# Right operands of a Strassen product summed in PSUM by identity passes, in a macaron block

## The chip, the cores and the metric

One core of one Trainium2 chip runs the kernel. The metric is the device time of one execution in microseconds (us); the time of a kernel is the median of its runs. A profile is one more execution, recorded by the hardware profiler; its span is the time from the first to the last recorded work.

## The reference

One layer on x of 1024 frames x 1024 channels, float32. Each feed-forward has 2816 inner channels.

```python
x = x + 0.5 * swiglu(rmsnorm(x, ff1_norm), ff1_w_gate, ff1_w_up, ff1_w_down)
h = rmsnorm(x, mix_norm)
...                      # gMLP and stick-breaking attention on h, merged, projected
x = x + m @ w_out
x = x + 0.5 * swiglu(rmsnorm(x, ff2_norm), ff2_w_gate, ff2_w_up, ff2_w_down)
return rmsnorm(x, final_norm)
```

`swiglu` is `(silu(x @ w_gate) * (x @ w_up)) @ w_down`, `rmsnorm` divides each row by its root mean square and multiplies by a gain.

## The kernel before

Every float32 product is made of three passes over operands split into a high and a low part (fp32r): high x high, high x low, low x high. A form is such a pair of parts; `form` (L152 to 157) makes one with a cast on ScalarE (L155) and a subtraction (L156), `put` (L186 to 191) makes one inside a larger tile, with the cast at L190 and the subtraction at L191.

The feed-forward (`ffn`) computes x @ w by a Strassen-Winograd scheme with seven products over 2 x 2 blocks. The right operand is the normed, transposed x: block B11 and B21 for rows 0 to 511 (the first and the second half of the channels), B12 and B22 for rows 512 to 1023, and four sums, T1 = B12 - B11, T2 = B22 - T1, T3 = B22 - B12, T4 = T2 - B21. Eight row tiles t of 128 rows are normed (`normed`, `rstd`), transposed on TensorE (`transposed`, L182) into two PSUM banks and written as forms: tiles 0 to 3 by `lo_forms` into B11 and B21, tiles 4 to 7 by `hi_forms` into T1 to T4 and B22. In the second feed-forward tiles 0 to 3 are formed by the mixer before it, at its end.

`hi_forms` first adds the high and the low part of B11 and B21 back together on GpSimd (two tiles "keep", L206), and then makes the four sums on VectorE, the first two out of PSUM (L209, L210), the others from SBUF (L213, L216). Of the five puts GpSimd does the subtraction of three (T1, T3, T4), VectorE of two (T2, B22).

A head is the part of an inner block f that needs B11 and B21 alone: two products of 12 passes each, into the banks b (from B11) and a (from B21); `head_end` adds them (L282, L283) and leaves b, into which the tail goes on accumulating. Four heads are computed between the tiles. Then come the tails, five products each, over T2, T1, T3, T4 and B22, for 22 inner blocks. Their left sums s1 to s4 (`sums`, from L163 on) are made by VectorE from the weights.

The down part multiplies by w_down with a second scheme; sums go through DRAM. Its last loop (`last`) runs products j = 0 to 10 into four banks A, one per tile t, of which the last five (j = 6 to 10) are done tile by tile; after each tile comes a sum (L490) and `after`, which norms a finished row tile. In the first feed-forward `after` also returns the transposing step `finish` (run as f() later, out of the list `lo`), in the second it stores the result.

In the stretches with the tiles 0 to 7 the order of TensorE and of the DMA queue (SyncE) is the order of the code (`manual_schedule`), in the last down loop that of TensorE; everything else is ordered by a planner that simulates the engines. All PSUM banks of a feed-forward come from one pool of 8. The parameter `offload` of `normed` says how many of a norm's two halves are multiplied by the gain on GpSimd (L116) and scaled on ScalarE (L120), the others being done on VectorE in one go (L122). With offload 2 the squares (L104) are written to a PSUM bank, otherwise to the norm's own first tile. The inverse root is a power on GpSimd (L108).

Of the kernel before, what the change touches and what calls it, by code (L numbers as in the profile page):

```python
# [7 lines left out]
F32 = mybir.dt.float32  # L8
# [5 lines left out]
P = 128  # L14
# [18 lines left out]
class Kernel:  # L33
# [77 lines left out]
    def normed(self, x, gain, tiles, offload):  # L111

        nc = self.nc
        far = [i for i in range(2) if i >= 2 - offload]
        for i in far:
            nc.gpsimd.tensor_tensor(tiles[i], x[i], gain[i], op=ALU.mult)  # L116
        r = self.rstd(x, self.psum("p3", "sq") if offload == 2 else tiles[0])
        for i in range(2):
            if i in far:
                nc.scalar.activation(tiles[i], tiles[i], AF.Copy, scale=r)  # L120
            else:
                nc.vector.scalar_tensor_tensor(tiles[i], x[i], r, gain[i], op0=ALU.mult, op1=ALU.mult)  # L122
# [10 lines left out]
    def norm_t(self, x, t, gain, h, offload=1):  # L133
# [3 lines left out]
        self.normed(x, gain, xns, offload)  # L137
# [39 lines left out]
    def transposed(self, xn):  # L177
        ps = []
        for i in range(2):
            p = self.psum("p2", "nt")  # L180
            for k in range(4):
                self.nc.tensor.transpose(p[:, k * P:(k + 1) * P], xn[i][:, k * P:(k + 1) * P], self.ident)  # L182
            ps.append(p)
# [15 lines left out]

    def hi_forms(self, t, xn, T, tmp):  # L200
        tt, pt = self.nc.vector.tensor_tensor, self.nc.gpsimd.tensor_tensor
        c, keep = (t % 4) * P, []
        for name in ("B11", "B21"):
            keep.append(tmp("keep", 2))
            hi, lo = (T[name][:, :, part, c:c + P].bitcast(F32) for part in range(2))
            pt(keep[-1].rearrange("p (k c) -> p k c", k=4), hi, lo, op=ALU.add)  # L206
        n = self.transposed(xn)
        t1, t2, t3, t4 = (tmp("t", 4) for _ in range(4))
        tt(t1, n[0], keep[0], op=ALU.subtract)  # L209
        tt(t2, n[1], t1, op=ALU.subtract)  # L210
        self.put(T["T2"], t, t2, tt)
        self.put(T["T1"], t, t1, pt)
        tt(t3, t2, keep[0], op=ALU.subtract)  # L213
        self.put(T["T3"], t, t3, pt)
        self.put(T["B22"], t, n[1], tt)
        tt(t4, t2, keep[1], op=ALU.subtract)  # L216
        self.put(T["T4"], t, t4, pt)

    def ffn(self, xsrc, gain_src, wg, wu, wd, before, after, T=None):
# [13 lines left out]
        with ExitStack() as outer:  # L233
# [16 lines left out]
            with tc.tile_pool(name="tp", bufs=3, reuse_waits="tile") as tp, tc.tile_pool(name="pg", bufs=1, reuse_waits="tile") as pg:  # L250
# [18 lines left out]
                def head(f, sub=None):  # L269
                    gate = weights(wg, f)  # L270
                    return [gate, [wform(g, sub) for g in gate], self.psum("ps", "pb"), None]

                def head_part(h, cs=slice(0, HALF)):
                    first = cs.start == 0
                    h[3] = h[3] or self.psum("ps", "pa")
                    passes(h[2], h[1][0], "B11", first, True, cs)
                    passes(h[3], h[1][1], "B21", first, True, cs)
# [8 lines left out]
                with tc.tile_pool(name="pre", bufs=1, reuse_waits="tile") as pre, tc.manual_schedule(engines={mybir.EngineType.PE, mybir.EngineType.SP}):  # L286
# [9 lines left out]
                    def norm(t):  # L296
                        xn = [tmp("xn", 4) for _ in range(2)]
                        self.normed(cut(x[t]), cut(gain), xn, 1)
# [5 lines left out]
                    if ready:  # L304
                        heads[0], heads[1] = head(0), head(1)
# [4 lines left out]
                    else:  # L310
# [102 lines left out]
            with tc.tile_pool(name="pb", bufs=1, reuse_waits="tile") as pb:  # L413
# [61 lines left out]
                with tc.manual_schedule(engines={mybir.EngineType.PE}):  # L475
                    lo = []
                    last(range(3), range(4))
# [3 lines left out]
                    for t in (0, 1):  # L481
                        lo.append(after(t, cut(x[t]), cut(gain), 2))
                    last(range(3, 5), range(4))
                    for f in lo:
                        f and f()
                    lo = [after(t, cut(x[t]), cut(gain), 2) for t in (2, 3)]
                    last(range(5, 6), range(4))
                    for t in range(4):
                        last(range(6, nj), [t], t == 0)
                        tt(xh(t + 4, 0), xh(t + 4, 0), A[t], op=ALU.subtract)  # L490
                        lo.append(after(t + 4, cut(x[t + 4]), cut(gain), 1))
                        f = lo.pop(0)
                        f and f()
# [213 lines left out]
    def run(self):  # L707
        nc, tc, a, ctx = self.nc, self.tc, self.a, self.ctx
        self.ident = self.const.tile([P, P], F32, name="ident")
        make_identity(nc, self.ident)  # L710
        self.neghalf = self.const.tile([P, 1], F32, name="neghalf")
# [11 lines left out]
        def after(t, x, gain, offload):  # L723
            for i in range(2):
                nc.sync.dma_start(out=xmid[t * P:(t + 1) * P, i * HALF:(i + 1) * HALF], in_=x[i])
            return self.norm_t(x, t, gain, hm, offload)
# [12 lines left out]
        def after3(t, x, gain, offload):  # L739
            xo = [self.np_.tile([P, HALF], F32, tag="xn", bufs=XNF, name="xo") for _ in range(2)]  # L740
            self.normed(x, gain, xo, offload)
# [5 lines left out]
    def mixer(self, xmid, xres, ydram, bgate):  # L747
# [7 lines left out]
        with tc.tile_pool(name="u2", bufs=42, reuse_waits="tile") as self.up, tc.tile_pool(name="np2", bufs=3, reuse_waits="tile") as self.np_:  # L755
# [56 lines left out]
            def after2(t):  # L812
                for i in range(2):
                    nc.sync.dma_start(out=xres[t * P:(t + 1) * P, i * HALF:(i + 1) * HALF], in_=x[t][i])
                if t < 4:
                    xn[t] = [self.utile("xn") for _ in range(2)]
                    self.normed(x[t], gain, xn[t], 1)
# [46 lines left out]
```

## Time and profile before

| | us |
|---|---|
| median of 3 runs (2554.43 to 2556.69) | 2554.93 |
| profiled execution | 2552.09 |
| span of its profile | 2550.3 |
| TensorE busy | 2429.8 |
| VectorE busy | 1716.0 |
| ScalarE busy | 1054.4 |
| GpSimd busy | 391.5 |

Matmuls are pipelined, and their ends are modelled: a pass of 512 columns is listed with 0.39 us, and the next one starts 0.23 us after it. The first feed-forward lies from 0 to about 720 us, with its tiles 0 to 7 up to about 76 us and its down part from about 420 us; the mixer follows to about 1868 us; the second feed-forward has its tiles 4 to 7 from there to about 1921 us. In the views PE is TensorE (PEld its weight loads), DVE is VectorE, ACT ScalarE, POOL GpSimd, SP SyncE; L171 to L173 are the three passes of a feed-forward product. In brackets behind a row of a timeline stands how long the engine was idle before it and what ended that.

### The profile page before, as it was taken

What the parts mean: (1) busy time and instruction counts of PE and PEld (TensorE: products, weight loads), DVE (VectorE), ACT (ScalarE), POOL (GpSimd) and SP (SyncE); (2) the same over time, 40 slices, a digit from 0 to 9 for tenths busy, and PEclk for the clock granted to TensorE, in tenths of its full rate; (3) what the DMA queues carried; (4) which work ended last, traced back from release to release, by engine and by line L of the source; (5) the groups of instructions that cost most, each with busy time, mean ns of one, the idle gap of its engine ahead of it and who ended that gap; (6) DMA issues with size and microseconds to landing.
All of it is one profiled execution on the core that took longest, in us unless ns stands there. A gap on an engine that the chain in (4) does not pass through costs nothing.

```text
span 2550.3 us, 33259 instructions
## 1 busy us (share of the span) xinstructions
PE 2429.8 (95%) x12188; PEld 2060.4 (81%) x12188; DVE 1716.0 (67%) x2605; ACT 1054.4 (41%) x2004; POOL 391.5 (15%) x538
## 2 busy tenths in 40 slices
PE   5899999999899999999999999999978999999998
PEld 4688888778798888888888988888857888887886
DVE  6877776565648888887666555135778777775655
ACT  5433333343546666665522222222343333333534
POOL 6100000000214444443300000000150000000003
PEclk9899999999999999999999999999999999999999
DMA  4454544775421212122111111123345535537653
GB/s 141 138 175 158 173 148 153 265 262 191 153 60 42 59 42 59 42 59 51 34 57 49 55 62 59 50 79 128 120 140 159 183 132 175 168 130 292 236 182 132
DMA packets 252771, 318.33 MB, mean 125 GB/s; under 512 B 14912, under 2 KB 172096, under 8 KB 252608
## 3 DMA queue, kind: packets, MB, share of 16 engines
q1 hardware_dynamic: 252608, 316.21, 38.3%
q8 instruction: 96, 1.57, 0.3%
q14 instruction: 67, 0.55, 0.1%
HBM read 227.55 MB, written 80.22 MB: 121 GB/s over the span
## 4 chain that ended last, share of the span: by engine, by line
PE 85%; DVE 5%; DMA 4%; issue 1%; ACT 1%; SPq 0%; POOL 0%; POOLq 0%; DVEq 0%; ACTq 0%
PE pj L67 7%; PE pj L68 7%; PE pj L69 7%; PE pd L171 7%; PE pd L172 7%; PE pd L173 7%; PE pb L171 4%; PE pb L172 4%; PE pb L173 4%; PE av L598 3%; PE tr L591 2%; PE pv L67 2%; PE pv L69 2%; PE pv L68 2%; PE pe L171 2%; PE pe L172 2%
## 5 line engine op out<-in xcount | busy, mean ns | idle before, releaser
L156 DVE TENSOR_TENSOR wf<-raw,wf 128x512 fp32r<-128x512 f32 x276 | 192.0, 717 | 121.3 <-ACT wf L155 121.2
L155 ACT CAST wf<-raw 128x512 fp32r<-128x512 f32 x280 | 166.2, 620 | 259.7 <-PE pd L173 128.4
L67 PE MATMUL pj<-h,wf 128*128 128x512 f32 x640 | 253.7, 396 | 5.3 <-DVE q L74 5.3
L68 PE MATMUL pj<-h,wf 128*128 128x512 f32 x640 | 252.9, 395 | 0.0
L69 PE MATMUL pj<-h,wf 128*128 128x512 f32 x640 | 252.2, 395 | 0.0
L574 DVE TENSOR_TENSOR_SCAN kp<-kp 128x128 f32<-128x128 f32 (+7 forms) x128 | 181.1, 1421 | 39.9 <-POOL kp L572 38.5
L57 DVE TENSOR_TENSOR wf<-raw,wf 128x1024 fp32r<-128x1024 f32 x88 | 108.3, 1231 | 143.8 <-ACT wf L56 143.3
L155 ACT CAST wf<-ws 128x512 fp32r<-128x512 f32 x176 | 106.6, 621 | 201.4 <-DVE ws L164 97.9
L56 ACT CAST wf<-raw 128x1024 fp32r<-128x1024 f32 x88 | 92.8, 1055 | 219.0 <-PE pj L68 116.7
L171 PE MATMUL pb<-T,wf 128*128 128x512 f32 x352 | 137.6, 391 | 34.2 <-ACT wf L155 34.2
L116 POOL TENSOR_TENSOR xn<-x,gain 128x512 f32<-128x512 f32 x16 | 23.0, 1463 | 883.4 <-DVE x L450 469.3
L578 POOL TENSOR_TENSOR bt<-bt,kp 128x512 f32<-128x512 f32 (+4 forms) x128 | 131.4, 1027 | 141.0 <-DVE kp L574 109.3
L67 PE MATMUL pv<-wf,h 128*128 128x256 f32 x512 | 145.2, 286 | 2.1 <-ACT vg L641 2.1
L67 PEld LDWEIGHTS pj<-h,wf 128*128 128x128 f32 x640 | 121.9, 190 | 30.0 <-DVE q L74 6.0
L69 PE MATMUL pv<-wf,h 128*128 128x256 f32 x512 | 145.3, 284 | 0.0
L68 PE MATMUL pv<-wf,h 128*128 128x256 f32 x512 | 145.1, 284 | 0.0
L69 PEld LDWEIGHTS pj<-h,wf 128*128 128x128 f32 x640 | 121.6, 190 | 25.1 <-DVE wf L57 0.2
L68 PEld LDWEIGHTS pj<-h,wf 128*128 128x128 f32 x640 | 121.7, 190 | 24.1
L172 PE MATMUL pb<-T,wf 128*128 128x512 f32 x352 | 137.5, 391 | 0.0
L173 PE MATMUL pb<-T,wf 128*128 128x512 f32 x352 | 136.8, 389 | 0.0
L172 PE MATMUL pd<-wf 128*128 128x512 f32 x344 | 134.6, 391 | 1.8 <-DVE wf L156 1.8
L171 PE MATMUL pd<-wf 128*128 128x512 f32 x344 | 132.8, 393 | 3.5 <-ACT wf L155 2.1
(215 smaller groups left out, 6600.2 us busy)
## 6 DMA issues: line engine op xcount, KB each, us to landing
raw<-in_ff_w_down_dram SPq DMA_DIRECT2D x66, 512.0 KB, 6.3
raw<-in_w_in_dram SPq DMA_DIRECT2D x56, 512.0 KB, 3.9
raw<-in_ff_w_gate_dram SPq DMA_DIRECT2D x52, 512.0 KB, 4.7
raw<-in_ff_w_up_dram SPq DMA_DIRECT2D x44, 512.0 KB, 6.2
f_t2t<-as SPq DMA_DIRECT2D x22, 512.0 KB, 3.2
f_a11a<-act SPq DMA_DIRECT2D x44, 256.0 KB, 4.4
f_s2s<-as SPq DMA_DIRECT2D x22, 512.0 KB, 2.7
f_s3s<-as SPq DMA_DIRECT2D x22, 512.0 KB, 5.7
```

Of the source, the lines that this page charges most:

```text
L56: nc.scalar.copy(hi, raw)
L57: (nc.gpsimd if early else nc.vector).tensor_tensor(lo, raw, hi.bitcast(F32), op=ALU.subtract)
L67: mm(ps, lhsT=lh, rhs=rh, start=first, stop=False)
L68: mm(ps, lhsT=lh, rhs=rl, start=False, stop=False)
L69: mm(ps, lhsT=ll, rhs=rh, start=False, stop=last)
L155: self.nc.scalar.copy(f[:, 0, :], src)
L156: (sub or self.nc.vector.tensor_tensor)(f[:, 1, :], src, f[:, 0, :].bitcast(F32), op=ALU.subtract)
L171: mm(ps, lhsT=lh, rhs=rh, start=first, stop=False, skip_group_check=True)
L172: mm(ps, lhsT=lh, rhs=rl, start=False, stop=False, skip_group_check=True)
L173: mm(ps, lhsT=ll, rhs=rh, start=False, stop=last, skip_group_check=True)
L574: nc.vector.tensor_tensor_scan(rev, rev, rev, 1.0, op0=ALU.mult, op1=ALU.bypass)
L578: eng.tensor_tensor(bt[:, :n], bt[:, :n], kp[:, i * HALF + 1:i * HALF + 1 + n], op=ALU.mult)
```

## The change

`hi_forms` no longer sums on VectorE. GpSimd makes one difference, diff = xn[1] - xn[0] (B22 - B12 before the transposes), TensorE transposes it into a third bank d (T3), and the other sums are made inside the banks by passes with a plus or minus identity over the forms of B11 and B21 (`plus`, two passes of 512 columns each): the bank of B12 minus B11 is T1, d plus B11 is T2, and after T2 has been put, d minus B21 is T4. All five puts read PSUM and have their subtraction on VectorE. `second` and `third` are these later steps; the heads are cut into their two products and placed between them, two of them moved by one tile in the first feed-forward. The subtractions of the head weights' forms go to GpSimd. Norms lose `offload`: always one half on GpSimd and ScalarE, the other on VectorE. In the last down loop norms 0 and 1 stand ahead of the eight adds (L479, L480), norm 2 ahead of j = 5, norm 3 ahead of j = 6, and the transposes follow one at a time.

```diff
+    def plus(self, ps, sign, form, t):
+        c = (t % 4) * P
+        for part in range(2):
+            self.nc.tensor.matmul(ps, lhsT=self.unit[sign], rhs=form[:, :, part, c:c + P], start=False, stop=True, skip_group_check=True)
     def hi_forms(self, t, xn, T, tmp):
-        tt, pt = self.nc.vector.tensor_tensor, self.nc.gpsimd.tensor_tensor
-        c, keep = (t % 4) * P, []
-        for name in ("B11", "B21"):
-            keep.append(tmp("keep", 2))
-            hi, lo = (T[name][:, :, part, c:c + P].bitcast(F32) for part in range(2))
-            pt(keep[-1].rearrange("p (k c) -> p k c", k=4), hi, lo, op=ALU.add)
-        n = self.transposed(xn)
-        t1, t2, t3, t4 = (tmp("t", 4) for _ in range(4))
-        tt(t1, n[0], keep[0], op=ALU.subtract)
-        tt(t2, n[1], t1, op=ALU.subtract)
-        self.put(T["T2"], t, t2, tt)
-        self.put(T["T1"], t, t1, pt)
-        tt(t3, t2, keep[0], op=ALU.subtract)
-        self.put(T["T3"], t, t3, pt)
-        self.put(T["B22"], t, n[1], tt)
-        tt(t4, t2, keep[1], op=ALU.subtract)
-        self.put(T["T4"], t, t4, pt)
+        tt = self.nc.vector.tensor_tensor
+        diff = tmp("diff", 2)
+        self.nc.gpsimd.tensor_tensor(diff, xn[1], xn[0], op=ALU.subtract)
+        b12, b22 = self.transposed(xn)
+        d = self.transposed([diff])[0]
+        self.put(T["B22"], t, b22, tt)
+        self.put(T["T3"], t, d, tt)
+        def second():
+            self.plus(b12, -1, T["B11"], t)
+            self.put(T["T1"], t, b12, tt)
+            self.plus(d, 1, T["B11"], t)
+            self.put(T["T2"], t, d, tt)
+        def third():
+            self.plus(d, -1, T["B21"], t)
+            self.put(T["T4"], t, d, tt)
+        return second, third
...
-                        heads[0], heads[1] = head(0), head(1)
+                        heads[0], heads[1] = head(0, pool), head(1, pool)
...
-                        work = {5: 2, 6: 3}
+                        work = {4: 2, 5: 3}
                     for t in range(4, NT):
+                        f = work.get(t)
+                        if f is not None and f not in heads:
+                            heads[f] = head(f, pool)
                         xn = norm(t)
-                        if t in work:
-                            f = work[t]
-                            if f not in heads:
-                                heads[f] = head(f)
-                            head_part(heads[f])
-                            full(f)
+                        if ready:
+                            head_part(heads[f], which=(2,))
+                        second, third = self.hi_forms(t, xn, T, tmp)
                         if t == 4:
                             load(7)
-                        self.hi_forms(t, xn, T, tmp)
+                        if f is not None:
+                            head_part(heads[f], which=(3,) if ready else (2,))
+                            if ready:
+                                full(f)
+                        second()
+                        if f is not None and not ready:
+                            head_part(heads[f], which=(3,))
+                            full(f)
+                        third()
...
-                    lo = []
-                    last(range(3), range(4))
+                    lo = [after(t, cut(x[t]), cut(gain)) for t in (0, 1)]
                     for t in range(4):
                         tt(xh(t + 4, 0), old[t], xh(t + 4, 0), op=ALU.add)
                         tt(xh(t + 4, 1), old[t], xh(t + 4, 1), op=ALU.add)
-                    for t in (0, 1):
-                        lo.append(after(t, cut(x[t]), cut(gain), 2))
-                    last(range(3, 5), range(4))
-                    for f in lo:
-                        f and f()
-                    lo = [after(t, cut(x[t]), cut(gain), 2) for t in (2, 3)]
+                    last(range(5), range(4))
+                    lo.append(after(2, cut(x[2]), cut(gain)))
+                    run = lambda f: f and f()
+                    run(lo.pop(0))
                     last(range(5, 6), range(4))
+                    lo.append(after(3, cut(x[3]), cut(gain)))
+                    run(lo.pop(0))
                     for t in range(4):
                         last(range(6, nj), [t], t == 0)
                         tt(xh(t + 4, 0), xh(t + 4, 0), A[t], op=ALU.subtract)
-                        lo.append(after(t + 4, cut(x[t + 4]), cut(gain), 1))
-                        f = lo.pop(0)
-                        f and f()
+                        lo.append(after(t + 4, cut(x[t + 4]), cut(gain)))
+                        run(lo.pop(0))
```

`ready` is true in the second feed-forward. A head's bank b is now taken at its first pass, not when its weights are loaded, and two tiles of 128 x 128 (plus and minus identity) are made once at the start.

## Rows read from the trace of the kernel before

**Rows 1.** The page's first part: busy time (share of span), instructions of TensorE.
```profile
PE 2429.8 (95%) x12188; PEld 2060.4 (81%) x12188; DVE 1716.0 (67%) x2605; ACT 1054.4 (41%) x2004; POOL 391.5 (15%) x538
```
**Rows 2.** TensorE's waits by releaser: us in total, times, longest.
```profile
PE pb L171 <- ACT wf L155: 34.2, 2, 17.5
```
**Rows 3.** Windows: stretch, length, each engine's busy time, granted clock, DMA.
```profile
52.00:76.00 24.00, 2.17 (x9) 1.80 (x10) 22.43 (x24) 10.59 (x17) 20.71 (x14) 0.55 0.05 14
678.00:700.00 22.00, 13.51 (x63) 10.96 (x62) 16.39 (x24) 16.72 (x33) 8.43 (x7) 0.77 0.49 154
1904.00:1921.00 17.00, 0.30 (x4) 0.06 (x2) 16.79 (x18) 6.72 (x13) 12.64 (x9) 0.61 0.06 18
```
**Rows 4.** TensorE's timeline, tiles of the first feed-forward: start, length, instruction, idle before.
```profile
21.61 1.09 PE L182 MATMUL nt<-ident,xn 128*128 128x128 f32 x8 [3.03 <-DVE xn L122]
...
34.51 1.03 PE L182 MATMUL nt<-ident,xn 128*128 128x128 f32 x8
...
42.21 1.03 PE L182 MATMUL nt<-ident,xn 128*128 128x128 f32 x8
43.00 0.48 PE L171 MATMUL pb<-B,wf 128*128 128x512 f32 x1
...
45.82 0.39 PE L171 MATMUL pa<-B,wf 128*128 128x512 f32 x1
...
56.33 1.94 PE L182 MATMUL nt<-ident,xn 128*128 128x128 f32 x8 [6.21 <-DVE xn L122]
75.77 0.80 PE L171 MATMUL pb<-T,wf 128*128 128x512 f32 x1 [17.50 <-ACT wf L155]
...
81.48 0.46 PE L171 MATMUL pe<-T,wf 128*128 128x512 f32 x1
```
**Rows 5.** VectorE's timeline, the same stretch.
```profile
59.02 1.75 DVE L191 TENSOR_TENSOR T<-t,T 128x512 fp32r<-128x512 f32 x1
60.69 0.68 DVE L191 TENSOR_TENSOR B<-nt,B 128x512 fp32r<-128x512 f32 x1
...
69.84 1.75 DVE L163 TENSOR_TENSOR ws<-raw 128x512 f32<-128x512 f32 x1
```
**Rows 6.** GpSimd's timeline, the same stretch.
```profile
16.73 2.55 POOL L206 TENSOR_TENSOR keep<-B 128x512 f32<-128x512 f32 x2
19.21 0.57 POOL L108 TENSOR_TENSOR rs<-rs,neghalf 128x1 f32<-128x1 f32 x1
...
65.99 6.72 POOL L191 TENSOR_TENSOR T<-t,T 128x512 fp32r<-128x512 f32 x4
```
**Rows 7.** ScalarE's timeline, the same stretch.
```profile
57.62 0.62 ACT L190 CAST T<-t 128x512 fp32r<-128x512 f32 x1 [0.17 <-DVE t L210]
```
**Rows 8.** TensorE's timeline, tiles of the second feed-forward.
```profile
1880.40 1.97 PE L182 MATMUL nt<-ident,xn 128*128 128x128 f32 x8 [5.35 <-DVE xn L122]
...
1920.97 0.79 PE L171 MATMUL pb<-T,wf 128*128 128x512 f32 x1 [16.70 <-ACT wf L155]
...
1924.90 0.40 PE L173 MATMUL pe<-T,wf 128*128 128x512 f32 x1
```
**Rows 9.** Timelines of ScalarE, TensorE and VectorE, end of the first down part.
```profile
686.67 0.60 ACT L104 ACTIVATE sq<-x 128x512 f32<-128x512 f32 x1 [1.72 <-DVE h L74]
695.24 1.97 PE L182 MATMUL nt<-ident,xn 128*128 128x128 f32 x8 [8.42 <-ACT xn L120]
...
699.50 0.40 PE L171 MATMUL pd<-pf 128*128 128x512 f32 x1
701.79 0.69 DVE L490 TENSOR_TENSOR x<-x,pd 128x512 f32<-128x512 f32 x1 [2.48 <-PE pd L173]
...
705.72 1.76 DVE L122 SCALAR_TENSOR_TENSOR xn<-x,rs,gain 128x512 f32<-128x512 f32 x1 [0.75 <-POOL rs L108]
```
**Rows 10.** Timelines of TensorE and VectorE, end of the kernel.
```profile
2540.46 0.39 PE L173 MATMUL pd<-wf 128*128 128x512 f32 x1
2541.68 0.68 DVE L490 TENSOR_TENSOR x<-x,pd 128x512 f32<-128x512 f32 x1
```

More of the change, by code (lines that the diff above doesn't have):

```diff
@@ L109, in rstd, with normed @@
         return r[:, 1:2]
-    def normed(self, x, gain, tiles, offload):
+    def normed(self, x, gain, tiles):
         nc = self.nc
[L114 to L122, printed above, removed]
+        nc.gpsimd.tensor_tensor(tiles[1], x[1], gain[1], op=ALU.mult)
+        r = self.rstd(x, tiles[0])
+        nc.vector.scalar_tensor_tensor(tiles[0], x[0], r, gain[0], op0=ALU.mult, op1=ALU.mult)
+        nc.scalar.activation(tiles[1], tiles[1], AF.Copy, scale=r)
     def gain(self, g):
@@ L178, in transposed @@
         ps = []
-        for i in range(2):
+        for x in xn:
             p = self.psum("p2", "nt")
             for k in range(4):
-                self.nc.tensor.transpose(p[:, k * P:(k + 1) * P], xn[i][:, k * P:(k + 1) * P], self.ident)
+                self.nc.tensor.matmul(p[:, k * P:(k + 1) * P], lhsT=x[:, k * P:(k + 1) * P], rhs=self.ident, is_transpose=True, start=k == 0, stop=True, skip_group_check=True)
             ps.append(p)
@@ L270, in head, with head_part @@
                     gate = weights(wg, f)
-                    return [gate, [wform(g, sub) for g in gate], self.psum("ps", "pb"), None]
-                def head_part(h, cs=slice(0, HALF)):
+                    return [gate, [wform(g, sub) for g in gate], None, None]
+                def head_part(h, cs=slice(0, HALF), which=(2, 3)):
                     first = cs.start == 0
-                    h[3] = h[3] or self.psum("ps", "pa")
-                    passes(h[2], h[1][0], "B11", first, True, cs)
-                    passes(h[3], h[1][1], "B21", first, True, cs)
+                    for n, right in ((2, "B11"), (3, "B21")):
+                        if n in which:
+                            h[n] = h[n] or self.psum("ps", "pba"[n - 2:n])
+                            passes(h[n], h[1][n - 2], right, first, True, cs)
                 def head_end(h):
@@ L297, in norm @@
                         xn = [tmp("xn", 4) for _ in range(2)]
-                        self.normed(cut(x[t]), cut(gain), xn, 1)
+                        self.normed(cut(x[t]), cut(gain), xn)
                         return xn
@@ L710, in run @@
         make_identity(nc, self.ident)
+        self.unit = {sign: self.const.tile([P, P], F32R, name=name) for sign, name in ((1, "plus"), (-1, "minus"))}
+        for sign, u in self.unit.items():
+            nc.vector.tensor_scalar(u, self.ident, float(sign), None, op0=ALU.mult)
         self.neghalf = self.const.tile([P, 1], F32, name="neghalf")
@@ L721, in run, with after @@
         hm = self.new_h()
-        def after(t, x, gain, offload):
+        def after(t, x, gain):
             for i in range(2):
                 nc.sync.dma_start(out=xmid[t * P:(t + 1) * P, i * HALF:(i + 1) * HALF], in_=x[i])
-            return self.norm_t(x, t, gain, hm, offload)
+            return self.norm_t(x, t, gain, hm)
         self.ffn(a["x"][0], a["ff1_norm"][0], a["ff1_w_gate"][0], a["ff1_w_up"][0], a["ff1_w_down"][0], a["mix_norm"][0], after)
@@ L737, in run, with after3 @@
         self.stage = "f2"
-        def after3(t, x, gain, offload):
+        def after3(t, x, gain):
             xo = [self.np_.tile([P, HALF], F32, tag="xn", bufs=XNF, name="xo") for _ in range(2)]
-            self.normed(x, gain, xo, offload)
+            self.normed(x, gain, xo)
             for i in range(2):
@@ L816, in after2 @@
                     xn[t] = [self.utile("xn") for _ in range(2)]
-                    self.normed(x[t], gain, xn[t], 1)
+                    self.normed(x[t], gain, xn[t])
             with tc.manual_schedule(engines={mybir.EngineType.PE}):
```

4 lines of the change are left out of this document (2 added, 2 removed).

## The prediction

> **What bounds the kernel now.** I read the share of each engine first: the matmul engine is busy 2429.8 of 2550.3 us [rows 1], so the change can only pay where that engine stands idle, 120 us in all. Then the list of what it waited for [rows 2]: 34.2 us in two waits on weight forms (L155); one more, of 8.42 us on xn by ScalarE, is in the timeline [rows 9]. The windows say where these lie [rows 3]. From 52 to 76 us (T forms of the first feed-forward) TensorE works 2.17 us of 24, VectorE 22.43 and GpSimd 20.71; from 1904 to 1921 us (the same in the second) TensorE 0.30 of 17, VectorE 16.79. The two waits, 17.5 and 16.7 us [rows 4, 8], are put down to a weight form, but that form stood behind the T work in VectorE's queue: its first sum (L163) starts at 69.84, when VectorE has done its last T sum, and runs straight on [rows 5]. So VectorE and GpSimd, by their T1 to T4 work, set the end of both stretches. The third place is 678 to 700 us, the end of the first down part, with TensorE at 13.51 of 22 and a clock of 0.77.
>
> **T sums in PSUM, cost on each engine.** Per right tile (t = 4 to 7, in two feed-forwards) VectorE loses four sums and one put and GpSimd two "keep" sums and three puts. In the trace a T put with both inputs in SBUF takes 1.75 us beside GpSimd, a put out of PSUM 0.68 in the same stretch [rows 5]; GpSimd's keeps cost 1.27 and its puts 1.7 each [rows 6]. Removed per tile: about 4 x 0.7 to 1.7 + 1.75 = 4.5 to 8.5 us of VectorE and 2 x 1.27 + 3 x 1.7 = 7.6 of GpSimd. Left: five puts out of PSUM, 5 x 0.68 = 3.4 us of VectorE, one new difference on GpSimd, taken as a keep, 1.27 (bound 1.7, a put beside a busy VectorE). ScalarE keeps its five casts of 0.6 [rows 7]. TensorE gains 4 transposes and 6 passes of 512 columns per tile. Eight transposes push the next operation by 0.79 and a half head of 12 passes by 2.8 [rows 4], so 12 transposes are 1.2 and 6 passes 6 x 0.23 = 1.4. No row shows a pass with plus or minus identity over a strided right operand: its nearest rows are the 0.23 step of this kernel's passes and, far off, the four fp32 transposes that also cover 512 columns, 0.4. I take 0.23, since type and width are those passes'; the bounds give 48 x 0.17 = 8 us more, and no gain, since passes are only added.
>
> **The new waits.** A pass into a bank must wait until the put of that bank's last value is done. After the transposes: cast of B22, cast of T3 (0.6 each), put of T3 0.68, then the pass for T2 (0.45 with both parts), cast and put of T2 (0.6 + 0.68), and only then the pass for T4. With hand-overs of some 0.1 to 0.2 (estimate from the gaps between such steps) T2's pass comes 1.7 us after the last transpose and T4's 3.8 after it. The order of TensorE is written by hand, so everything for the next tile stands behind that wait.
>
> **First feed-forward.** Before, tile 4's transposes start at 34.51 and the products at 75.77 [rows 4]. New, counted from 34.51: tiles 4 and 5 have a head between their steps, which covers the waits: 1.2 + 2.72 + 0.9 + 2.72 + 0.45 = 8.0 each, to 50.5. Tiles 6 and 7 have none: 1.2 + 3.8 + 0.45 = 5.45 each. T2 of tile 7 is there at 50.5 + 5.45 + 5.0 = 61.0, T4's pass ends at 61.4. Those two waits of tiles 6 and 7 go through ScalarE's and VectorE's queues, where casts and puts of 0.6 stand between; I add 0.6 for each of four, 2.4 us. Ahead of it, norm 2's power (L108) starts at 19.21 only because GpSimd did the two keeps from 16.73 on [rows 6], and the transposes waited 3.03 us for it [rows 4]; without the keeps I take 2 us (bounds 0 and 2.5). Start of products: 61.4 + 2.4 - 2 = 61.8, 14 us earlier. The form of s2 must be there too: from L163 two sums, a cast and a put are 2.7 us, which VectorE can do in its new idle time; if the planner puts them last, 2.7 is lost. Weights of head 2 are now asked for ahead of x of tile 7; x 7 is needed only some 20 us later, at tile 7's transposes, so I cost that at nothing; with this cover gone tile 7 would wait for its whole norm, about 6 us [rows 9]. Finally the products start at half clock today, 13 steps from 75.77 to 81.48 [rows 4], 5.7 us where 13 x 0.23 = 3.0 would do, so 2.7 us; with pauses under 2 us this may vanish. I take half, 1.3. First feed-forward: 15.3, bounds 8 and 19.
>
> **Second feed-forward.** Here every tile has a head, but nothing stands between the second and the third pass, so each tile waits about 1.7 us. Tile 4's transposes can't come before 1880.40 [rows 8], since x 4 must land; the first half head lies ahead of it, the other half goes behind. Tile 4: transposes 2.5 (cold, with the wait on the difference), 3.3, 0.9, 1.7, 0.45, to about 1889.3; tiles 5 to 7: 2.72 + 1.2 + 2.72 + 0.9 + 1.7 + 0.45 = 9.7 each, so T4's last pass ends at 1918.4 and the products can start then, against 1920.97. So the 16.7 us of idle time here turn mostly into TensorE work that was done earlier or is new (24 passes, 16 transposes, a half head moved, four waits). Add 0.6 of queueing for each of four waits, -2.4, and the cold start that goes (9 steps from 1920.97 to 1924.90 [rows 8], 3.9 us for 2.1, so 1.8). Net 1.9, bounds -6 and 5. Heads 0 to 3 now have their low parts made by GpSimd, 1.27 instead of 0.68, in time that GpSimd had idle or spent on keeps; cost nothing, 2.5 if it delays tile 4's difference.
>
> **Order of the last norms.** In the first down part, norm 2 is issued after tiles 0 and 1 have been transposed, and its squares go to a PSUM bank: ScalarE's first square waits for it until 686.67, and TensorE stands idle for 8.42 us until 695.24, with the transposes and six passes after it at half speed: 4.3 us from 695.24 to 699.50 where 0.79 + 6 x 0.23 = 2.2 would do [rows 9]. Now its squares go to the norm's own tile and it is issued before passes j = 5; x 2 is final before norms 0 and 1 are, in the adds that end the third product pair. Its transposes stay at the same place in TensorE's order, so 8.4 + 2.1 = 10.5 us go. VectorE gets one product per norm more (0.75), GpSimd one fewer (1.27); VectorE makes the weight forms there too, and if one comes late by the three products that norms 0 to 2 add at 0.75 or 1.76 [rows 9], 2 to 5 us are lost: bounds 5 and 11. Next late would be norms 4 to 7: last sum to xn is about 6 us (701.79 to 707.5), the transposes come two groups and two sets of transposes later, 2 x (3.4 + 0.8) = 8.4: no wait. In the last down part TensorE transposes nothing; the last pass starts at 2540.46 and lasts 0.39, the last sum starts at 2541.68 [rows 10], so at most 0.8 is won, and a form that comes later costs as much. Taken at 0, bounds -2 and 1.
>
> **Sum.** 15.3 + 1.9 + 10.5 = 27.7 us off the profiled 2552.1 gives 2524.4. The median is 2554.93, 2.8 above the profiled run; the same saving gives 2527.
>
> **A rule against it.** Rows: a gap of 3.03 us left the clock at its upper level of 2.4 GHz (transposes x8 in 1.09), gaps of 5.35 and 6.21 us dropped it to 1.2 GHz (1.97, 1.94) [rows 4, 8]. My gaps are 1.3 to 1.7 us, but there are eight, some after little work. The Trainium skill, page "TensorE: Matmul & The Clock Gate", section "A second HAM failure mode: psum-queue depth-cycling", says that a kernel that steps through PSUM banks with small pauses between its groups of matmuls can swing between both levels. The trace neither shows nor excludes that for pauses this short. By the rows alone the sum stands; by the rule it is the third rival.
>
> **Rivals.** *Late puts.* The planner orders ScalarE and VectorE by itself; if squares, head copies and weight casts stand ahead of the puts, each of the eight T2 and T4 waits that no head covers (four in tiles 6 and 7 of the first, one a tile in the second) grows by two casts or squares of 0.6 and a put, 1.8 us, 14 us in all, and 2541 results. For it: ScalarE keeps all its casts and they are now on the path; against it: VectorE and GpSimd lose half their work there. *Norms still late.* Norm 2 or 3 is queued behind the adds and forms and the wait only shrinks: 5 to 8 us back, 2533. *Half clock (slower).* If all matmuls from tile 4 to the products run at 1.2 GHz: second feed-forward 7 x 12 + 24 passes at 0.2 more and 48 transposes at 0.1 more, 26 us; first 72 passes and the transposes, 19; together 45, so 2572. It turns the sign from some 60% of that stretch at half clock. *Passes slow.* If a pass with identity ran at a quarter of the rate, 48 x 0.68 = 33 us more, 2560; type and width speak against it. *Better than forecast.* No queueing in the waits (4.8), no cold start in the first products (1.4), a last sum without delay (0.8): 2520; the upper bounds of all terms together, 19 + 5 + 11 + 1 = 36, give 2519.
>
> **Chances.** Forecast 0.55 (2522 to 2532), better 0.10, norms late 0.12, late puts 0.14, half clock 0.05, slow passes 0.04. The range reaches from 2517 to 2543: below to the upper bounds, 2 us spared for the spread of the runs, above over late puts. A difference under 0.2%, 5 us, can't be told from none; late puts together with late norms reach into that. Faster 0.87, same 0.05, slower 0.08.
>
> **What would show it.** Right: products of the first feed-forward start near 62, of the second near 1918 minus what was won before, at full clock; no wait of 8 us before the transposes of tile 2; waits of 1 to 2 us before the new helper's passes. Wrong: granted clock under 0.9 between tile 4 and the products, gaps of 3 us before the passes, or a form of s2 that TensorE waits for after T2 is done.

## The result and the profile after

The changed kernel takes 2538.31 us (median of 4 runs, 2534.12 to 2541.97) against 2554.68 for the kernel before (4 runs, 2551.73 to 2556.69): a ratio of 0.9936 with an interval of 0.9918 to 0.9955. That is 16.4 us faster, where 27.7 were forecast. The profiled execution took 2541.97 us, the longest of its four, 10.1 us below the profiled execution of before. Two more profiles of each kernel, told of below, took 2539.92 and 2541.03 us (changed) and 2551.9 and 2551.96 (before), so 11.0 us lie between the means of the profiled executions; the median of a repeat with four runs is 12.0 us below that of before. The accounts below are made from the profiles; what the first medians show beyond it is the spread of the runs.

The first part of the page, as [rows 1], of the changed kernel:

```profile
PE 2451.0 (96%) x12268; PEld 2074.1 (82%) x12268; DVE 1685.2 (66%) x2595; ACT 1050.4 (41%) x1996; POOL 350.0 (14%) x510
```

TensorE is busy for 21 us more, VectorE for 31 less, GpSimd for 42 less. So the work did move as the change says, and TensorE's idle time fell from 120 to 89 us.

TensorE's waits by releaser (us in total, times, longest); the first line is the stretch from 0 to 90 us, the next two are 1840 to 1960 us:

```profile
PE nt L199 <- DVE T L186: 6.0, 4, 2.2
...
PE nt L199 <- DVE T L186: 8.5, 3, 4.7
PE nt L177 <- DVE xn L116: 7.7, 1, 7.7
```

The 34.2 us on weight forms [rows 2] are gone but for 0.8 and 1.2 us before the first products. In their place stand waits of the identity passes (L199) for VectorE's puts (L186), seven in all, of 1.1 to 4.7 us.

Where the time went, from TensorE's timelines: the start of the n-th pass of a product (identity passes and transposes not counted) is set against the mean of the three profiles of before, and a stage's entry is by how much that difference changed across it, in us. Where three numbers stand, they are the three profiles of the changed kernel.

| stage | forecast | before, its own three | changed | sums alone | norms alone |
|---|---|---|---|---|---|
| first feed-forward, tiles to products | -15.3 | -0.5 to +0.4 | -9.9, -9.7, -9.5 | -10.8 | -0.2 |
| its products, and down part up to the norms | 0 | 0.0 | -0.5, -1.5, -1.4 | -0.7 | -0.7 |
| norms of the first down part | -10.5 | -0.2 to +0.3 | -9.1, -8.9, -9.3 | +0.5 | -8.9 |
| mixer | 0 | -1.3 to +1.1 | +1.0, +0.6, -1.2 | -0.2 | +1.4 |
| second feed-forward, tiles to products | -1.9 | -0.2 to +0.3 | +5.5, +4.9, +4.4 | +5.4 | -0.8 |
| its products and last down part | 0 | -0.6 to +1.1 | +3.2, +3.6, +7.2 | +1.7 | +2.3 |
| sum | -27.7 | | -9.8, -10.9, -9.7 | -4.1 | -6.8 |

"Sums alone" and "norms alone" are the first two experiments.

### The profile page after: what moved, and what is told of

It reads as the page before. It is cut to its first block, busy times and chain, and to the rows that moved or that the text cites. A ratio compares the mean times of both kernels' runs of the same rounds, so it can differ in the third digit from the quotient of the medians.

```text
span 2540.2 us, 33329 instructions
## 1 busy us (share of the span) xinstructions
PE 2451.0 (96%) x12268; PEld 2074.1 (82%) x12268; DVE 1685.2 (66%) x2595; ACT 1050.4 (41%) x1996; POOL 350.0 (14%) x510
## 4 chain that ended last, share of the span: by engine, by line
PE 83%; DVE 7%; DMA 4%; issue 2%; ACT 1%; POOL 1%; SPq 0%; POOLq 0%; DVEq 0%; ACTq 0%
PE pj L67 7%; PE pj L68 7%; PE pj L69 7%; PE pd L168 7%; PE pd L167 7%; PE pd L166 7%; PE pb L167 4%; PE pb L166 4%; PE pb L168 4%; PE av L609 3%; PE pv L68 2%; PE pv L69 2%; PE pv L67 2%; PE tr L602 2%; PE pe L167 1%
## 5 line engine op out<-in xcount | busy, mean ns | idle before, releaser
L151 DVE TENSOR_TENSOR wf<-raw,wf 128x512 fp32r<-128x512 f32 x264 | 178.0, 696 | 118.0 <-ACT wf L150 115.7
L114 POOL TENSOR_TENSOR xn<-x,gain 128x512 f32<-128x512 f32 x12 | 16.8, 1406 | 893.9 <-DVE x L474 601.6
```

Source lines behind the costliest of these rows:

```text
L151: (sub or self.nc.vector.tensor_tensor)(f[:, 1, :], src, f[:, 0, :].bitcast(F32), op=ALU.subtract)
```

## Experiments

**One part at a time.** "Sums alone" leaves the norms and the last down loop as they were; "norms alone" is the kernel before with these lines:

```diff
-    def normed(self, x, gain, tiles, offload):
+    def normed(self, x, gain, tiles):
...
-                    last(range(3, 5), range(4))
-                    for f in lo:
-                        f and f()
-                    lo = [after(t, cut(x[t]), cut(gain), 2) for t in (2, 3)]
+                    last(range(5), range(4))
+                    lo.append(after(2, cut(x[2]), cut(gain)))
+                    run = lambda f: f and f()
+                    run(lo.pop(0))
```

> The T sums in PSUM alone; norms and last down loop as before. Theory 1 (the two parts are independent, and the second feed-forward loses): the first feed-forward gains some 10 us, the second loses 5 to 6 between tile 4 and the products, the 8.4 us wait before the transposes of tile 2 in the first down part stays; 2548 to 2551 us. Rival (the T sums gain in both places and the norms gave nothing): 2538 us, as the whole change.

> The order of the last norms alone (and the norm without offload); T sums as before. Theory 1: the wait of 8.4 us before the transposes of tile 2 goes, with the half-speed passes behind it, and about 1 to 2 us come back as a later wait for tile 4 and a late weight form in the last down part; 2554.7 - 9 = 2545 to 2547 us. Rival (the gain there came from the T sums, or the wait only moves): 2552 us or more.

Measured: sums alone 2547.81 us (10 runs) against 2552.79 (13 runs of before), ratio 0.9982 (0.9973 to 0.9992); norms alone 2542.62 (4 runs), 0.9961 (0.9946 to 0.9976). Together 5.0 + 10.2 = 15.2 us, about the whole change's 16.4 (12.0 in the repeat), and in the table 4.1 + 6.8 = 10.9: the parts add up. Both times lie below what was expected, norms alone by 2.4 us; neither rival holds. The sums in PSUM, forecast at 17.2 of the 27.7 us, bring 5: what they win in the first feed-forward they lose by half in the second. TensorE's timeline at the end of the first down part, first of sums alone, then of norms alone:

```profile
684.37 1.97 PE L182 MATMUL nt<-ident,xn 128*128 128x128 f32 x8 [9.40 <-ACT xn L120]
```
```profile
689.38 1.06 PE L177 MATMUL nt<-ident,xn 128*128 128x128 f32 x8 [0.28 <-DVE xn L116]
695.55 1.09 PE L177 MATMUL nt<-ident,xn 128*128 128x128 f32 x8 [1.66 <-DVE xn L116]
```

With the old order the 8.42 us of [rows 9] stay (9.40); with the new order they are gone without the sums, and a wait of 1.66 comes up for tile 4.

**Both kernels again.** The changed kernel with nothing altered, timed on another chip:

> The whole change once more, for a second trace and more times: 2538 us, in the spread of 2534 to 2542 seen so far. If the attention stage, in which the first trace gave back 2.8 us, is slower because its order has changed, it is so again; if that was scatter between executions, it is not.

Measured: 2539.74 us (4 runs, 2536.34 to 2541.26) against 2551.74 (7 runs), ratio 0.9949 (0.9933 to 0.9966). Set against the first profile of before alone, most of these kernels lost 1 to 2.7 us in the mixer, whose code is the same in all. So both kernels were profiled once more:

> The kernel before, unchanged, profiled once more. Compared pass by pass with its first profile, all eight kernels tried so far lie behind by 0.1 to 2.7 us over the mixer and (but for none) by 0.6 to 2.6 us over the second feed-forward's products and last down part, though the mixer's code is the same in all of them. Theory 1, the first profile of the kernel before was a favourable execution: this profile is itself 1 to 3 us behind the first one over the mixer, and 0.5 to 2 us over the last stretch, and its time lies near 2554 to 2556. Theory 2, the change costs time there (other buffers, later requests): this profile agrees with the first within 0.5 us in both stretches, near 2552. The tiles of both feed-forwards and the norms of the first down part should agree within 1 us by either.

> The same as the run ahead of it, to see how far two profiles of the kernel before differ by stage. By theory 1 the mixer and the last stretch scatter by 1 to 3 us between three profiles of one kernel; by theory 2 all three agree within 0.5 us.

> The changed kernel, a third profile, on the chip of the two runs ahead of it. Against the mean of the three profiles of the kernel before: by theory 1 less than 1 us is lost over the mixer, by theory 2 2 to 3 us, as in the two profiles so far. Either way the tiles of the second feed-forward lose 5 to 6 us, the norms give 9.2 to 9.4, the tiles of the first feed-forward give 10.

Measured: before 2551.9 and 2551.96 us, changed 2541.03 us, one run each. Over the mixer the two new profiles of before are 2.4 and 1.5 us longer than the first, and the three of the changed kernel scatter by 2.2 us around the mean of before: the first theory holds, and nothing is lost in the mixer. In the other stretch neither theory holds whole. From 2304 to 2425 us of before its two new profiles are 1.6 and 1.4 us shorter than the first, not longer, and the third of the changed kernel is 4.1 longer than that first; its granted clock there is 0.96 against 0.99, and why is not explained. But over the last 79 passes of products (from 2516 us of before on) the three of before agree within 0.1 us, and the three of the changed kernel are 2.0, 2.7 and 2.6 us longer: that belongs to the change. So do the 4.4 to 5.5 us lost at the tiles of the second feed-forward.

**What stops tile 4 of the second feed-forward.** There the third step's pass waits 4.66 us. TensorE's timeline in the changed kernel, then ScalarE's in the same stretch:

```profile
1862.16 1.97 PE L177 MATMUL nt<-ident,xn 128*128 128x128 f32 x8 [7.71 <-DVE xn L116]
...
1868.32 0.63 PE L199 MATMUL nt<-B,plus 128*128 128x512 f32 x2
1873.60 1.22 PE L199 MATMUL nt<-B,minus 128*128 128x512 f32 x2 [4.66 <-DVE T L186]
1874.62 0.63 PE L166 MATMUL pb<-B,wf 128*128 128x512 f32 x1
...
1879.44 1.04 PE L177 MATMUL nt<-ident,xn 128*128 128x128 f32 x8
```
```profile
1867.48 1.14 ACT L150 CAST wf<-raw 128x512 fp32r<-128x512 f32 x2 [1.02 <-DMA raw<-in_ff_w_gate_dram]
1869.58 1.14 ACT L150 CAST wf<-raw 128x512 fp32r<-128x512 f32 x2 [0.96 <-DMA raw<-in_ff_w_gate_dram]
1870.62 0.72 ACT L117 ACTIVATE xn<-xn,rs 128x512 f32<-128x512 f32 x1
1871.25 1.05 ACT L185 CAST T<-nt 128x512 fp32r<-128x512 f32 x2
```

The sum for T2 is in its bank by about 1869, but ScalarE casts T1 and T2 only at 1871.25. Until then it stands, in order, at the casts of head 2's weights, which wait for their DMA (1.02 and 0.96 us idle), and at a scaled copy of the next norm. The test asks for those weights and forms them ahead of tile 4:

```diff
 for t in (4, 5, 6):
     load(t)
+heads[2], heads[3] = head(2, pool), head(3, pool)
```

> The whole change; in the second feed-forward the weights of heads 2 and 3 are asked for and made into forms ahead of tile 4's work, not during it. Theory 2 (T1 and T2 of tile 4 stand on ScalarE behind casts that wait for those weights, and the clock falls in that wait): the wait before tile 4's last pass falls from 4.7 to about 1.7 us, the half head behind it runs at 0.23 a pass, and 5 to 6 us are won against the whole change: 2532 to 2534 us. Rival (the wait is the chain of cast, put and pass itself): the wait stays over 4 us and the time at 2538.

Measured: 2535.84 us (4 runs), ratio 0.9936 (0.992 to 0.9953). TensorE's timeline:

```profile
1870.38 0.74 PE L199 MATMUL nt<-B,minus 128*128 128x512 f32 x2 [1.53 <-DVE T L186]
...
1873.71 1.03 PE L177 MATMUL nt<-ident,xn 128*128 128x128 f32 x8
...
1900.96 0.50 PE L166 MATMUL pd<-T,wf 128*128 128x512 f32 x1 [1.25 <-ACT wf L150]
```

The wait falls from 4.66 to 1.53 us, and from tile 4's transposes (1861.68) to the products it is 39.3 us, where the changed kernel took 1906.67 - 1862.16 = 44.5 (45.1 in the repeat, 40.6 before). So the weights, asked for and formed in that stretch, are shown as the cause, and of the stage's loss of 4.4 to 5.5 us only 0.4 is left; that they act through the queue on ScalarE is read from its timeline. The time was expected at 2532 to 2534 us and missed that: the ratio is that of the change's first four runs, so the whole time shows the gain of the stage only against the repeat (0.9949).

**The wait itself, covered by the next head.** The third step of a tile is issued behind the first half head of the next:

```diff
-                        second, third = self.hi_forms(t, xn, T, tmp)
+                            third()
+                        second, new = self.hi_forms(t, xn, T, tmp)
...
-                        third()
+                        third = new
+                        if not ready or t == NT - 1:
+                            third()
```

> The whole change; in the second feed-forward the last passes of tile t (T4) are issued behind the first half head of tile t + 1. If the waits before these passes are what the second feed-forward pays (4.7, 2.3, 1.5 us and the half clock behind the first), a half head of 2.7 us covers all but about 2 us of the first, and 5 to 7 us are won: 2532 us. If the second feed-forward is bound by what comes after (the sums of the first product's left operand, T2 of tile 7), the products start no sooner and 2538 stays.

Measured: 2530.16 us (4 runs), ratio 0.9914 (0.9899 to 0.9928). TensorE's timeline:

```profile
1873.60 0.73 PE L199 MATMUL nt<-B,minus 128*128 128x512 f32 x2 [2.22 <-DVE T L186]
1874.17 1.04 PE L177 MATMUL nt<-ident,xn 128*128 128x128 f32 x8
...
1881.96 0.62 PE L199 MATMUL nt<-B,minus 128*128 128x512 f32 x2
...
1897.49 0.50 PE L166 MATMUL pd<-T,wf 128*128 128x512 f32 x1 [1.25 <-ACT wf L150]
```

The late casts are still there, and T2 is put as late as in the changed kernel (the pass starts at 1873.60 in both), but TensorE has 2.7 us of a head to do meanwhile; the later third steps wait for nothing. 1862.06 to 1897.49 is 35.4 us, 9.1 less than with the change, and the stage gains 2.1 where that lost 4.4 to 5.5.

**What the pause does to the clock.** In the changed kernel the half head behind the wait of 4.66 us takes 1874.62 to 1879.44, 4.8 us, with steps of 0.43; the same twelve passes take 2.7 at full clock (in the two further profiles of the changed kernel the half head behind waits of 4.11 and 4.17 us takes 3.8 and 3.7). To part the pause from the late put, twelve spare passes were put between the second and the third step of tile 4 in the second feed-forward; their product is read by nobody:

```diff
+                        if ready and t == 4:
+                            passes(self.psum("ps", "dm"), spare, "B21", True)
                         third()
```

> The whole change with twelve spare passes (a product that nobody reads) on TensorE between the second and the third pass of tile 4 in the second feed-forward, where it idles 4.7 us at the end of which the clock has fallen. If the pause is what halves the clock, the wait shrinks by 2.7 us, ends at the same time, and the half head behind it runs at 0.23 a pass, 2.7 us, not 5.0: the products start 2 us earlier though work was added. If the clock falls for another reason, the half head stays at 5.0 us and nothing is won.

Measured: 2533.56 us in one run (before: 2551.74). TensorE's timeline:

```profile
1866.03 0.40 PE L166 MATMUL dm<-B,wf 128*128 128x512 f32 x1
...
1870.41 0.73 PE L199 MATMUL nt<-B,minus 128*128 128x512 f32 x2 [1.46 <-DVE T L186]
1870.98 0.39 PE L166 MATMUL pb<-B,wf 128*128 128x512 f32 x1
...
1873.71 1.04 PE L177 MATMUL nt<-ident,xn 128*128 128x128 f32 x8
```

The pass starts 11.5 us after tile 4's transposes (1858.93), as in the changed kernel (11.4): useless work did not bring the put forward. But the half head behind it now takes 2.7 us. So the pause, not the late put, costs the clock, 2.1 us against the first profile and 1.0 to 1.1 against the other two, beside the time of the wait; this rests on one run. That the whole run is 6 us shorter than the median of the change beside it can't be credited to this: tile 4 to the products takes 42.1 us instead of 44.5, and the rest lies in stretches that scatter from profile to profile.

**All waits filled.** The order of TensorE was written out anew: T is a tile's norm, transposes and first puts, s its second step, l its third, "h" one half of a head, "w" the forms of its weights. In the first of two kernels this is done in the second feed-forward alone, with the weights of heads 2 and 3 early; in the other also in the first.

```diff
+order = ([("h", 0, 2), ("h", 0, 3), ("T", 4), ("h", 1, 2), ("s", 4), ("h", 1, 3), ("T", 5), ("l", 4), ("h", 2, 2), ("s", 5),
+          ("T", 6), ("l", 5), ("h", 2, 3), ("s", 6), ("T", 7), ("l", 6), ("h", 3, 2), ("s", 7), ("h", 3, 3), ("l", 7)] if ready else
+         [("w", 2), ("T", 4), ("w", 3), ("h", 2, 2), ("s", 4), ("T", 5), ("l", 4), ("h", 2, 3), ("s", 5),
+          ("T", 6), ("l", 5), ("h", 3, 2), ("s", 6), ("T", 7), ("l", 6), ("s", 7), ("h", 3, 3), ("l", 7)])
```

> The whole change with weights 2 and 3 early, and the order of TensorE in the second feed-forward changed: both halves of head 0 ahead of tile 4's transposes (where TensorE idles 7.7 us), the other six halves where a put is waited for, the last passes of a tile behind the transposes of the next. The T4 to products stretch is then 12 transposes x 4, 24 passes and six half heads, some 28 us, where the whole change takes 44.5. If only waits and clock are in the way, the products start 12 to 15 us earlier and the time is 2538 - 13 = 2525 us. If VectorE or ScalarE then sets the end (five puts and a norm a tile are 5 us on each), some 8 us are won: 2530.

> As the run before, and in the first feed-forward too the four half heads stand one a tile, the last behind tile 7's second passes, so that the products start without a wait and at full clock. Against the run before: 3 to 5 us (the 5.7 us of half-speed passes at the start of the products, 2.7 of them lost, and a wait of 2.2), 2521 us. If norms 6 and 7 come too late for their transposes, nothing is won there.

Measured: 2521.73 us (4 runs), ratio 0.9882 (0.9868 to 0.9897), with the second alone; 2518.41 (4 runs, 2516.73 to 2518.73), 0.9867 (0.9852 to 0.9882), with both. TensorE's timeline of the latter, the longest wait of an identity pass in the first feed-forward and the last one there, the first pass of the products, and the longest wait of an identity pass in the second, at tile 5's third step:

```profile
43.84 0.73 PE L199 MATMUL nt<-B,minus 128*128 128x512 f32 x2 [2.58 <-DVE T L186]
...
58.84 0.73 PE L199 MATMUL nt<-B,plus 128*128 128x512 f32 x2 [1.93 <-DVE T L186]
...
63.74 0.39 PE L166 MATMUL pb<-T,wf 128*128 128x512 f32 x1
...
1872.51 0.73 PE L199 MATMUL nt<-B,minus 128*128 128x512 f32 x2 [1.36 <-DVE T L186]
```

By stages as in the table, the second feed-forward's tiles give 10.5 and 10.3 us where the change lost 4.4 to 5.5, and the first's 14.1, its products starting at full clock, where the change gained 9.5 to 9.9. This is faster than both kernels, by 33 us against the one before. The sums in PSUM can thus bring 14.1 + 10.3 = 24.4 us, more than the 17.2 of the forecast; the change as made leaves them in uncovered waits. No run has the heads placed so in the kernel before, so the part of the 24.4 us that is due to the order alone is not shown; against a large one speaks that VectorE is busy in that kernel's first feed-forward for 38.58 of the 41.26 us from tile 4's transposes to the products.

## Why the prediction was right or wrong

The time fell within the range (2517 to 2543), and faster was right. The likeliest case, 2527, was not what happened: of the 27.7 us forecast 16.4 came by the first medians, 12.0 by the repeat and 11.0 by the profiles. 2538 lies nearest to the rival *late puts*, 2541, but its mechanism is only part of the cause: of its eight waits two grew clearly, tile 4's in the second feed-forward and tile 7's in the first, and the rest of the shortfall lies elsewhere, so that the numbers agree so well is partly luck. Two of the signs set for being wrong came: a gap of over 3 us before a pass (4.66), and a granted clock under 0.9 between tile 4 and the products (0.89 in the second feed-forward; 0.92 in the first).

- **What bounds the kernel** held. Both waits of some 17 us went when VectorE and GpSimd lost the sums, and no wait of that size took their place: the longest behind tile 4's transposes is the 4.66 us for a put (ahead of them TensorE waits 7.71 us in the second feed-forward, 5.35 before).
- **Cost of a pass** held. The two passes of a step push the next operation by 0.46 us (47.43 to 47.90 in the rows below), 0.23 each; the rival *slow passes* is out. Puts out of PSUM take 0.68, GpSimd's difference 1.27, as taken.
- **First feed-forward, 15.3 forecast, 9.5 to 9.9 measured** (10.3 against the first profile of before, whose rows stand ahead of the prediction). TensorE's timeline there:

```profile
19.82 1.04 PE L177 MATMUL nt<-ident,xn 128*128 128x128 f32 x8
33.10 1.04 PE L177 MATMUL nt<-ident,xn 128*128 128x128 f32 x8
...
47.43 0.63 PE L199 MATMUL nt<-B,minus 128*128 128x512 f32 x2
47.90 0.62 PE L199 MATMUL nt<-B,plus 128*128 128x512 f32 x2
...
54.64 0.73 PE L199 MATMUL nt<-B,plus 128*128 128x512 f32 x2 [1.10 <-DVE T L186]
56.77 1.22 PE L199 MATMUL nt<-B,minus 128*128 128x512 f32 x2 [1.40 <-DVE T L186]
57.79 1.91 PE L177 MATMUL nt<-ident,xn 128*128 128x128 f32 x8
62.86 0.99 PE L199 MATMUL nt<-B,plus 128*128 128x512 f32 x2 [2.17 <-DVE T L186]
64.63 0.80 PE L166 MATMUL pd<-T,wf 128*128 128x512 f32 x1 [0.78 <-ACT wf L150]
...
70.11 0.39 PE L166 MATMUL pd<-T,wf 128*128 128x512 f32 x1
```

  The keeps on GpSimd were where the 3.03 us came from: the transposes start at 19.82 without a wait, 1.8 us earlier (2 taken). The products start at 64.63, not 61.8. Tile 4 took 10.2 us to tile 5 (43.34) instead of 8.0, with a wait of 1.33 us for T3's put that I had covered with a half head; tile 7's pass for T2 came 5.1 us after its transposes, where 1.2 + 1.7 + 0.6 = 3.5 were taken. VectorE says why:

```profile
60.31 0.69 DVE L406 TENSOR_TENSOR as<-raw 128x512 f32<-128x512 f32 x1 [0.38 <-issue]
60.92 0.68 DVE L408 TENSOR_TENSOR as<-raw 128x512 f32<-128x512 f32 x1
61.52 0.68 DVE L186 TENSOR_TENSOR B<-nt,B 128x512 fp32r<-128x512 f32 x1
62.12 0.68 DVE L186 TENSOR_TENSOR T<-nt,T 128x512 fp32r<-128x512 f32 x1
```

  The planner set two sums of w_down's blocks (L406, L408), which the down part needs much later, ahead of the two puts: my step had casts and puts in the queue, not these. The trace of before could have told it, since VectorE makes the same two sums there, in the midst of the first left sums:

```profile
71.51 1.75 DVE L393 TENSOR_TENSOR as<-raw 128x512 f32<-128x512 f32 x1
73.18 0.68 DVE L395 TENSOR_TENSOR as<-raw 128x512 f32<-128x512 f32 x1
```

  Then 1.3 us for a shorter cold start did not come: 64.63 to 70.11 is 5.5 us at half clock for ten passes, as 5.7 for thirteen before. The granted clock fell at tile 6's last step (1.22 for its two passes) and was down at tile 7's transposes (1.91). Windows (stretch, length, busy time of PE, PEld, DVE, ACT, POOL, granted clock, DMA share, GB/s):

```profile
52.00:65.00 13.00, 7.55 (x33) 5.17 (x31) 9.27 (x16) 8.18 (x15) 0.00 (x0) 0.80 0.18 50
65.00:70.00 5.00, 4.59 (x10) 2.93 (x10) 4.42 (x9) 1.13 (x3) 0.00 (x0) 0.50 0.89 277
...
1880.00:1907.00 27.00, 21.91 (x110) 17.39 (x108) 15.26 (x26) 12.86 (x27) 3.40 (x3) 1.00 0.10 29
```

  The Trainium skill, page "TensorE: Matmul & The Clock Gate", section "A second HAM failure mode: psum-queue depth-cycling", tells of a clock that swings between its two levels where a kernel cycles through PSUM banks and TensorE idles briefly between groups of matmuls. The trace agrees where tiles 6 and 7 have steps of their own and pauses of 1.1 to 2.2 us alone: the granted clock is 0.50 from 56.4 to 59.7 us, 1.00 from 59.8 to 63.1 and 0.50 from 63.2 to 69.9. From 1880 to 1907 us pauses of 2.31 and 1.53 us lie between half heads, and in this profile the clock stays at 1.00; but in the profile of the repeat it falls behind the same pause (granted clock 0.57 from 1886 to 1890 us):

```profile
1885.11 0.73 PE L199 MATMUL nt<-B,minus 128*128 128x512 f32 x2 [2.30 <-DVE T L186]
...
1886.87 0.63 PE L167 MATMUL pb<-B,wf 128*128 128x512 f32 x1
```

  It falls so in the third profile and with the sums alone too. Half clock as a rival for the whole stretch did not occur.
- **Second feed-forward, 1.9 forecast, 4.4 to 5.5 lost.** This is the step that failed most. Between the two profiles whose rows are shown it is 5.7 lost, so 7.6 us beside the forecast, in two places (0.4 us are won ahead of tile 4). From tile 4's transposes to the products I had 40.4 us with queueing, and it took 44.5: tile 4 up to its third step 12.5 instead of 8.9, since I counted weight casts on ScalarE as no more than 0.6 each and not the wait for the weights that such a cast carries; tile 5 12.9 instead of 9.7, 2.1 of it the half clock behind the pause; tile 6 10.0, 0.3 more than taken. The rest, 3.9, is at the first products: I let the cold start of 1.8 us go, but the early products wait 0.32 and 0.70 us for the low parts of T and of a weight form, and from 1910 to 1913 us run at half clock again. The early weights remove the first of these, as shown.
- **Order of the norms, 10.5 forecast, 8.9 to 9.3 measured.** The wait of 8.42 us is gone, and the transposes of tile 2 (675.01) come without one. "No wait" for norms 4 to 7 was wrong by 1.66 us:

```profile
685.64 1.09 PE L177 MATMUL nt<-ident,xn 128*128 128x128 f32 x8 [1.66 <-DVE xn L116]
```
```profile
677.62 1.70 DVE L116 SCALAR_TENSOR_TENSOR xn<-x,rs,gain 128x512 f32<-128x512 f32 x1
679.25 0.68 DVE L502 TENSOR_TENSOR x<-x,pd 128x512 f32<-128x512 f32 x1
```

  The sum that makes x 4 final (L502) stands behind norm 3's product on VectorE, which took 1.70 us beside GpSimd. I had priced these products for weight forms only, not for that sum.
- **Last down part, 0 forecast, 2.0 to 2.7 lost in its last 79 passes.** VectorE and TensorE there:

```profile
2515.30 2.37 DVE L151 TENSOR_TENSOR pf<-raw,pf 128x512 fp32r<-128x512 f32 x2
```
```profile
2517.73 0.79 PE L167 MATMUL pd<-pf 128*128 128x512 f32 x1 [1.93 <-DVE pf L151]
2518.32 0.63 PE L168 MATMUL pd<-pf 128*128 128x512 f32 x1
...
2530.38 0.39 PE L168 MATMUL pd<-wf 128*128 128x512 f32 x1
```

  A form came 1.93 us late, as two subtractions took 2.37 us while GpSimd multiplied a gain (L114, 1.63 us from 2514.89); the bound of 2 held only about. But late forms alone are the smaller part: the kernel before waits there too (0.81 and 1.32 us, against 0.77 and 1.93), and most of the 2.0 us is the half clock behind the wait, with passes 0.43 apart from 2518.32 to 2520.45, which the prediction did not have here. With the early weights, where the norms are the same, that form is 1.44 us late, the clock stays at 1.00 and only 0.5 us is lost:

```profile
2511.76 0.50 PE L167 MATMUL pd<-pf 128*128 128x512 f32 x1 [1.44 <-DVE pf L151]
```

  From the last pass to the end it is 9.8 us as before. With the norms alone the same 79 passes lose 2.0, with the sums alone nothing (-0.2), so it comes with the norms; that GpSimd's product is what slows the form is read from the timeline, not tested.
- **Mixer, 0 in the prediction by silence**, and 0 within the scatter of the profiles.

## What to carry to other kernels

Sums of an operand can go to TensorE as identity passes into PSUM at the price of ordinary passes, but each then turns into a chain of pass, cast, subtraction, pass; whether it pays depends on independent matmuls in TensorE's order behind every step (here some 5 us as made, 24.4 with heads placed in the waits). When an engine off the path comes onto it, list all that its queue holds in that stretch, and for each entry what it waits for: a short cast that waits for a DMA holds up the put behind it for the time of the DMA. A pause of TensorE is to be priced with what the clock does after it, and that in more than one profile.

## What the runs showed of the hardware

After a pause of 4.66 us in the second feed-forward (4.11 and 4.17 in the two further profiles, 4.02 with the sums alone) the clock was at 1.2 GHz in all four: in the first nearly all of the next twelve passes ran 0.43 us apart, in the others about five. With a pause of 1.46 us there and twelve passes ahead of it they ran at 2.4 GHz, 0.23 apart, in the one run made. After pauses of 2.2 to 2.6 us with half heads around them the clock stayed at 2.4 GHz in the first profile of the change and in the kernels with early weights, late third steps and all waits filled; after one of 2.30 or 2.31 us it fell in the two further profiles of the change and with the sums alone. In the first feed-forward pauses of only 1.10 and 1.40 us, with a few transposes and identity passes between them, were followed by 1.2 GHz. So the length of a pause alone does not say what the clock does: the work around it counts, and one and the same kernel does not show the same in each execution.
